# Requests for twelve weight loads moved to ScalarE's queue, and four splitting steps taken off VectorE

## The chip, the cores and the metric

The kernel runs on one core of a Trainium2 chip. The core has five engines that run side by side, each through its own list of instructions in order: TensorE (PE in the profile, its weight loads PEld), VectorE (DVE), ScalarE (ACT), GpSimd (POOL) and SyncE (SP), which here only requests transfers between the chip's memory and the on-chip memory. The metric is the device time of one execution in microseconds; lower is better.

## The reference

One layer of a bidirectional hybrid encoder over 512 tokens of width 1024. What matters here is the mixer: one combined input projection, whose columns feed a gated DeltaNet branch, an mLSTM branch and sigmoid gates.

```python
hn = rmsnorm(h_res, norm_mix_g) * (1.0 + sc1) + sh1        # 512 x 1024
proj = hn @ w_in                                           # 1024 x 6208 weights
a_qkv, a_z, a_gates, b_qk, b_v, b_o, b_gates, merge = split(proj)
...                                                        # DeltaNet: per chunk of 64 tokens, 8 heads
sol = triangular_solve(lower + eye, rhs, unit_diagonal=True)
...                                                        # o_a and h_b: the two branches
gate_a, gate_b = split(sigmoid(merge))                     # 2 x 1024 columns of proj
y = gate_a * (o_a @ w_branch_a) + gate_b * (h_b @ w_branch_b)
h_res = h_res + gt1 * (y @ w_out)
h_res = h_res + gt2 * hierarchical_moe(adaLN(h_res))       # 32 experts, 2 per token
```

All numbers are float32.

## The kernel before

The projection is worked in 48 tiles of 128 weight columns; a tile is named by its first column (w4416 is columns 4416 to 4543). For each tile `load_w` (L221 on) requests 512 KB of weights into a raw buffer (L224), splits them into a high part, rounded to TensorE's shorter float format (`move`, so L143 on ScalarE, L145 on VectorE or GpSimd), and a low part, raw minus high (`both`, L150). `proj_tile` (L340) then runs 24 matmuls of 512 columns: high weights by high inputs (L347), high by low (L348), low by high (L349). There are two raw, two high and two low buffers, so the request of a tile waits for the low part of the tile two before, and its high part waits for the matmuls of the tile two before.

A table of choices, `CHOICE`, says for each step which engine takes it: `hiw4672` is the high part of tile w4672, `low4672` its low part, "v" VectorE, "g" GpSimd, "a" ScalarE; a key that is missing takes the default, ScalarE for high parts and GpSimd for low parts. Every request for a load goes to SP's list.

A gate tile (`gate_tile`, L545) is a projection tile whose result goes through a tanh on ScalarE (L548, which frees one of the two PSUM accumulators) and is stored (L551) for later use. `GORDER` takes gate tiles 4 to 15 first: they are w4160, w4288, w4416, w4544, w4672, w4800, w4928, w5056, w5184, w5312, w5440 and w5568. In the program's text these twelve stand at the head of the part after the DeltaNet preparation, but a scheduler that works with estimated durations lists the instructions of each engine, and it mixes the twelve tiles with three other things:

- the end of the DeltaNet preparation: `vt` (L582), `gg` and `ib` (L671, L672), their stores `gd` and `iqd` (L673, L597), and the exchange, that is, transposes on TensorE (L608) whose results ScalarE and VectorE copy from PSUM into `kst` and `vp` (L143, L147);
- the triangular solve on VectorE: `gu` is loaded back from `gd` (L720), four steps make `nn` (L729, L731), then 31 pairs of a product into `gu` (L740) and an addition into `tt` (L742), and six transposes into `tw` (L752) end it;
- the modulation columns `mod_chunk`: weights `aw` (L781) by a per-partition scalar, added up in `ac` on VectorE (L788, L790), or, for one chunk here, on ScalarE (L786) and VectorE (L792 to L796); then a small matmul (L800) and a copy into `mcols` (L801).

After the solve come `bx` (L982, L983), the low part of w5696 on VectorE (L150), and with it TensorE's next projection tiles.

Of the kernel before, what the change touches and what calls it, by code (L numbers as in the profile page):

```python
# [110 lines left out]
def _body(tc, nc, ctx, ins, out, consts_in):  # L111
    V, A, G, PE, DMA = nc.vector, nc.scalar, nc.gpsimd, nc.tensor, nc.sync
    x, w_in, ada_w = ins["x"][0], ins["w_in"][0], ins["ada_w"][0]
# [13 lines left out]
    def ps(tag, shape=None):  # L127
        uid[0] += 1
        n, b = psum["tags"][tag]
        return psum["pool"].tile([128, n], F32, name=f"ps_{tag}{uid[0]}", tag=tag, bufs=b)  # L130
# [6 lines left out]
    def nb(key, default, *choices):  # L137
        return eng("#" + key, default, (default,) + choices)

    def move(key, dst, src, scale=None, default="a", choices="av"):  # L140
        e = eng(key, default, choices)
        if e == "a":
            A.activation(dst, src, AF.Copy, **({} if scale is None else {"scale": scale}))  # L143
        elif scale is None:
            ENGINE[e].tensor_copy(dst, src)  # L145
        else:
            ENGINE[e].tensor_scalar(dst, src, scale, None, op0=OP.mult)  # L147

    def both(key, dst, a, b, op, default="v", choices="vg"):
        ENGINE[eng(key, default, choices)].tensor_tensor(dst, a, b, op=op)  # L150
# [67 lines left out]

    RAWP = nb("wraw", 2, 3)

    def load_w(src, n, name, first=False):  # L221
        raw = ppr.tile([128, KD, 128], F32, name=name + "_raw", tag="wraw", bufs=RAWP)
        for (s, o, m) in src:
            DMA.dma_start(raw[:, :, o:o + m], s.rearrange("(k p) n -> p k n", p=128))  # L224
        if not first:
            hi = ppr.tile([128, KD, 128], F32R, name=name + "_hi", tag="whi", bufs=nb("whi", 2, 3))
            lo = ppr.tile([128, KD, 128], F32R, name=name + "_lo", tag="wlo", bufs=nb("wlo", 2, 3))
        else:
            hi, lo = (pf.tile([128, KD, 128], F32R, name=f"{name}_{i}") for i in range(2))
        move("hi" + name, hi[:, :, :n], raw[:, :, :n], choices="avg")  # L230
        both("lo" + name, lo[:, :, :n], raw[:, :, :n], hi[:, :, :n].bitcast(F32), OP.subtract, "g")
        return hi, lo
# [5 lines left out]
    def early_w(i):  # L238
        if i == 0:
            early[i] = load_w([(w_in[:, 2048:2080], 0, 32), (w_in[:, 4128:4160], 32, 32)], 64, "wg"), 64  # L240
        else:
            c0 = EARLY[i - 1]
            early[i] = load_w([(w_in[:, c0:c0 + 128], 0, 128)], 128, f"w{c0}", i > 1), 128
# [30 lines left out]
    for k in range(KD):  # L274
        p = ps("m")
# [48 lines left out]
    for nm, n in (("gdn_conv_w", 12), ("mlstm_conv_w", 8)):  # L324
        w = p0.tile([128, KD, 2, 256], F32, name="cwr" + nm, tag="adaw", bufs=3).rearrange("p k b n -> p (k b n)")
# [3 lines left out]
    p = ps("m")  # L329
# [7 lines left out]

    unprojected = [48]

    def proj_tile(c0):  # L340
        unprojected[0] -= 1
        if c0 in EARLY:
            return ep[1 + EARLY.index(c0)]
        hi, lo = load_w([(w_in[:, c0:c0 + 128], 0, 128)], 128, f"w{c0}")
        p = ps("acc")
        for k in range(KD):
            PE.matmul(p, hi[:, k], hn_hi[:, k], start=(k == 0), stop=False)  # L347
            PE.matmul(p, hi[:, k], hn_lo[:, k], start=False, stop=False)  # L348
            PE.matmul(p, lo[:, k], hn_hi[:, k], start=False, stop=(k == KD - 1))  # L349
        return p  # L350

    p = ep[0]
# [43 lines left out]
    p = ps("m")  # L396
# [13 lines left out]
    for c in range(2):  # L410
        p = ps("m")
# [17 lines left out]
    p = ps("m")  # L429
# [15 lines left out]
    for n in range(NCH):  # L445
        for d in range(2):
            i = n if d == 0 else NCH - 1 - n
# [95 lines left out]
    gts = dram("gts", [20, 128, S])  # L543

    def gate_tile(i):  # L545
        p = proj_tile(1536 + i * 128 if i < 4 else 4160 + (i - 4) * 128)
        th = cv.tile([128, S], F32, name=f"gt{i}", tag="ct", bufs=nb("ct", 2, 3))
        A.activation(th, p, AF.Tanh, scale=0.5)  # L548
        if i < 4:
            V.scalar_tensor_tensor(th, th, 1.0, p, op0=OP.add, op1=OP.mult)  # L550
        DMA.dma_start(gts[i], th)  # L551

    def gate_tiles():
        for i in GORDER:
            gate_tile(i)
            yield
# [66 lines left out]
    def gdn_pair(hp):  # L623
# [7 lines left out]
        for j, col0 in ((0, 512), (1, 0)):  # L631
            p = proj_tile(col0 + hp * 128)
            nm = f"{j}_{hp}"
            ac = conv_tile(p, (4 if j == 0 else 0) + hp, nm)
            silu2(kq[:, j], ac, nm)
            yield
# [44 lines left out]
    def gdn_value(hp):  # L681
        p = proj_tile(1024 + hp * 128)
        nm = f"v{hp}"
        ac = conv_tile(p, 8 + hp, nm)
        vt = pa.tile([128, S], F32, name=f"vt{hp}", tag="vt", bufs=nb("vt", 2, 3))
        silu2(vt, ac, nm)
        yield
        exchange(token_blocks(vt), put_scaled(vp[:, hp], 0.5, f"v{hp}"))
# [48 lines left out]
    for c in range(31):  # L737
        n, m = 31 - c, c + 1
        o = pd[:, :, :n * m].rearrange("p b (i j) -> p b i j", j=m)
# [9 lines left out]
    for i, (own, kind) in enumerate(((True, 0), (False, 1), (True, 1))):  # L749
        for d in range(2):  # L750
            m = tt[halves[d], d if own else 1 - d]
# [351 lines left out]
    p = ps("m")  # L1103
# [162 lines left out]
    def weight_tile(nm):  # L1266
        return pw.tile([128, 2048], F32, name="wr" + nm, tag="wraw", bufs=RAW)
# [84 lines left out]
    p = ps("m")  # L1352
# [8 lines left out]
    p = ps("m")  # L1361
# [163 lines left out]
    for i in range(2 * NT):  # L1525
        (c, t), (c1, t1) = divmod(i, NT), divmod(i - 1, NT)
        p = ps("acc")
# [146 lines left out]
    for i, (n, w) in enumerate(((64, 512), (64, 512), (32, 256), (32, 256), (32, 256), (32, 256))):  # L1674
        r, c, o = ((i, 0, i * 512) if i < 2 else (i - 2, 512, (i - 2) * 256))
# [79 lines left out]
    def t32(nm, n=32):  # L1755
        return px.tile([128, n], F32, name=nm)
# [4 lines left out]
    first = t32("first")  # L1761
# [185 lines left out]
    with tc.For_i(0, nblk, 1) as i:  # L1947
# [23 lines left out]
        c0 = t32("c0", NT)  # L1971
# [12 lines left out]
        raw = [weight_tile(f"v_{c}") for c in range(3)]  # L1984
# [14 lines left out]
        p = ps("m")  # L1999
# [4 lines left out]
        p = ps("d")  # L2004
# [88 lines left out]
```

## Time and profile before

| | us |
|---|---|
| median of 3 runs (lowest, highest) | 983.03 (981.76, 984.24) |
| the profiled execution, device time | 980.42 |
| its span in the profile | 978.6 |
| busy in the span: PE, DVE, ACT, POOL | 814.2, 660.8, 328.1, 316.6 |

The profile is of one execution and has the times of single instructions; the shares of busy time are averages over stages that differ much. The span is 1.8 us shorter than the device time of the same execution, and that execution was 2.6 us below the median of the three runs. Of the span, the part that the change touches lies between 140 and 290 us. Times in the views are microseconds from the start of the span.

### The profile page before, as it was taken

What the parts mean: (1) busy time and instruction counts of PE and PEld (TensorE: products, weight loads), DVE (VectorE), ACT (ScalarE), POOL (GpSimd) and SP (SyncE); (2) the same over time, 40 slices, a digit from 0 to 9 for tenths busy, and PEclk for the clock granted to TensorE, in tenths of its full rate; (3) what the DMA queues carried; (4) which work ended last, traced back from release to release, by engine and by line L of the source; (5) the groups of instructions that cost most, each with busy time, mean ns of one, the idle gap of its engine ahead of it and who ended that gap; (6) DMA issues with size and microseconds to landing.
All of it is one profiled execution on the core that took longest, in us unless ns stands there. A gap on an engine that the chain in (4) does not pass through costs nothing.

```text
span 978.6 us, 16538 instructions
## 1 busy us (share of the span) xinstructions
PE 814.2 (83%) x6204; PEld 595.0 (61%) x6204; DVE 660.8 (68%) x1246; ACT 328.1 (34%) x611; POOL 316.6 (32%) x236
## 2 busy tenths in 40 slices
PE   4799979979486999988797998987699999999840
PEld 3367656768375777866675776776456555555420
DVE  1459999799959999888888888459965322221215
ACT  5435475223101342321334231125522323333203
POOL 0321365214224442563236252323112212111125
PEclk9799999989786999998898999998899999999985
DMA  9932564975265365654474254946689999999965
GB/s 307 270 88 71 108 119 97 204 206 180 58 143 158 87 216 146 181 171 142 150 220 149 94 157 132 369 166 215 237 288 358 351 371 403 414 417 413 415 259 211
DMA packets 171709, 213.80 MB, mean 218 GB/s; under 512 B 47368, under 2 KB 129828, under 8 KB 171628
## 3 DMA queue, kind: packets, MB, share of 16 engines
q1 hardware_dynamic: 167340, 204.33, 64.6%
q0 software_dynamic: 4288, 8.41, 2.4%
q8 instruction: 49, 0.80, 0.3%
q14 instruction: 32, 0.26, 0.1%
HBM read 190.79 MB, written 25.54 MB: 221 GB/s over the span
## 4 chain that ended last, share of the span: by engine, by line
PE 41%; DVE 31%; DMA 16%; issue 5%; POOL 3%; ACT 2%; SPq 1%; POOLq 0%; DVEq 0%; ACTq 0%
DMA wr<-in_w_gate_dram 5%; PE ps_m L1705 5%; DMA wr<-in_w_up_dram 4%; PE ps_acc L348 3%; PE ps_acc L347 3%; PE ps_acc L349 3%; DMA wr<-in_w_down_dram 3%; DVE gu L740 2%; PE ps_m L1708 2%; PE ps_d L1736 2%; DVE ac L790 2%; DVE tt L742 2%; DVE ca L573 1%; PE ps_m L902 1%; DMA hb<-h1d 1%
## 5 line engine op out<-in xcount | busy, mean ns | idle before, releaser
L349 PE MATMUL ps_acc<-hn_hi,w_lo 128*128 128x512 f32 x352 | 142.6, 405 | 16.2 <-DVE w_lo L150 15.4
L347 PE MATMUL ps_acc<-hn_hi,w_hi 128*128 128x512 f32 x352 | 145.5, 413 | 1.8 <-DVE w_hi L145 1.3
L348 PE MATMUL ps_acc<-hn_lo,w_hi 128*128 128x512 f32 x352 | 145.0, 412 | 0.0
L1705 PE MATMUL ps_m<-wr,xin 128*64 128x256 f32 x1024 | 124.4, 390 | 6.1 <-ACT xin L1695 4.2
L150 POOL TENSOR_TENSOR w_lo<-w_raw,w_hi 128x1024 fp32r<-128x1024 f32 x34 | 88.1, 2590 | 103.2 <-ACT w_hi L143 80.9
L1714 DVE SCALAR_TENSOR_TENSOR act<-act,ps_m 64x256 f32<-64x256 f32 (+1 forms) x32 | 14.8, 463 | 133.0 <-ACT act L1713 133.0
L1705 PEld LDWEIGHTS ps_m<-wr,xin 128*64 128x64 f32 x1024 | 75.0, 139 | 43.3 <-issue 6.8
L349 PEld LDWEIGHTS ps_acc<-hn_hi,w_lo 128*128 128x128 f32 x352 | 68.7, 195 | 32.1 <-DVE w_lo L150 16.6
L347 PEld LDWEIGHTS ps_acc<-hn_hi,w_hi 128*128 128x128 f32 x352 | 68.8, 196 | 17.5 <-issue 3.2
L348 PEld LDWEIGHTS ps_acc<-hn_lo,w_hi 128*128 128x128 f32 x352 | 68.8, 195 | 15.6 <-issue 1.5
L1752 POOL DMA_INDIRECT ybuf<-y,idxp x28 | 27.3, 974 | 132.7 <-DVE y L1747 123.8
L1736 PE MATMUL ps_d<-wr,at 128*64 128x512 f32 x256 | 61.3, 598 | 5.2 <-DMA wr<-in_w_down_dram 4.0
L1695 ACT ACTIVATE xin<-xall (+1 forms) x128 | 54.2, 424 | 13.8 <-issue 9.5
L1713 ACT ACTIVATE act<-ps_m 64x256 f32<-64x256 f32 (+1 forms) x32 | 13.4, 418 | 134.7 <-PE ps_m L1705 71.1
L143 ACT ACTIVATE w_hi<-w_raw 128x1024 fp32r<-128x1024 f32 x30 | 31.7, 1058 | 57.3 <-PE ps_acc L348 43.5
L790 DVE SCALAR_TENSOR_TENSOR ac<-aw,cT,ac 128x256 f32<-128x256 f32 x77 | 44.0, 572 | 0.6
L1752 POOL DMA_INDIRECT ybuf<-y,idx x16 | 15.9, 992 | 74.6 <-DVE y L1747 61.1
L1747 DVE TENSOR_TENSOR y<-ps_d,gt 128x512 f32<-128x512 f32 (+1 forms) x32 | 25.3, 792 | 21.4 <-PE ps_d L1736 16.7
L1736 PEld LDWEIGHTS ps_d<-wr,at 128*64 128x64 f32 x256 | 17.4, 136 | 30.0 <-issue 20.1
L1725 PEld LDWEIGHTS ps_m<-ident,act 64*128 64x128 f32 x128 | 16.5, 186 | 22.4 <-DVE act L1715 12.6
L1497 PE MATMUL ps_acc<-woh,yT 128*128 128x512 f32 x64 | 27.5, 430 | 0.0
L740 DVE TENSOR_TENSOR gu<-nn,tt 128x62 f32<-128x62 f32 (+15 forms) x31 | 27.0, 870 | 0.7
(550 smaller groups left out, 1788.0 us busy)
## 6 DMA issues: line engine op xcount, KB each, us to landing
wr<-in_w_gate_dram SPq DMA_DIRECT2D x64, 512.0 KB
wr<-in_w_up_dram SPq DMA_DIRECT2D x64, 512.0 KB
wr<-in_w_down_dram SPq DMA_DIRECT2D x32, 1024.0 KB
w_raw<-in_w_in_dram SPq DMA_DIRECT2D x48, 512.0 KB
aw<-in_ada_w_dram SPq DMA_DIRECT2D x32, 512.0 KB
adaw<-in_ada_w_dram SPq DMA_DIRECT2D x8, 1024.0 KB
gts<-gt SPq DMA_DIRECT2D x20, 256.0 KB
gts<-gts SPq DMA_DIRECT2D x20, 256.0 KB
```

What stands on the lines that cost most here:

```text
L143: A.activation(dst, src, AF.Copy, **({} if scale is None else {"scale": scale}))
L150: ENGINE[eng(key, default, choices)].tensor_tensor(dst, a, b, op=op)
L347: PE.matmul(p, hi[:, k], hn_hi[:, k], start=(k == 0), stop=False)
L348: PE.matmul(p, hi[:, k], hn_lo[:, k], start=False, stop=False)
L349: PE.matmul(p, lo[:, k], hn_hi[:, k], start=False, stop=(k == KD - 1))
L740: V.tensor_tensor(o, nn_[:, :, m:, c].unsqueeze(3).to_broadcast([128, 2, n, m]), tt[:, :, c, 0:m].unsqueeze(2).to_broadcast([128, 2, n, m] ...
L790: V.scalar_tensor_tensor(acc, w[:, k], cT[:, kk:kk + 1], acc, op0=OP.mult, op1=OP.add)
L1497: PE.matmul(p, yT[0][:, k, ts], hi[:, k % 2], start=(k == 0), stop=False)
L1695: A.activation(xg[:, :, o], xall[:, :, bass.ds(vs[t], SEG)], AF.Copy)
L1705: PE.matmul(p[64 * b:64 * b + 64, 0:256], xg[:, kk, 0:64], r[:, b], **f)
L1736: PE.matmul(p[64 * c:64 * c + 64, 0:512], at[:, j, 0:64], w[:, j * D + c * 512:j * D + c * 512 + 512], start=(j == 0), stop=(j == 1))
L1752: return G.indirect_dma_start(out=ybuf.rearrange("r (a n) -> (r a) n", a=parts), out_offset=bass.IndirectOffsetOnAxis(ap=ix, axis=0), in_= ...
```

## The change

Twelve gate tiles, 4 to 15, hand `nc.scalar` down to `load_w`, so that their loads are requested from ScalarE's list in place of SP's. Four keys leave the table: `hiw4672` goes from VectorE to ScalarE, and `low4416`, `low4672` and `low4928` go from VectorE to GpSimd. One blank line is added in `gate_tile`, so lines from L546 on have a number higher by one in the changed kernel.

```diff
-    "hiw4544": "g", "hiw4672": "v", "hiw5824": "v", ...
+    "hiw4544": "g", "hiw5824": "v", ...
-    "low3744": "v", "low4416": "v", "low4672": "v", "low4928": "v", "low5696": "v", ...
+    "low3744": "v", "low5696": "v", ...
-    def load_w(src, n, name, first=False):
+    def load_w(src, n, name, first=False, queue=None):
...
-            DMA.dma_start(raw[:, :, o:o + m], s.rearrange("(k p) n -> p k n", p=128))
+            (queue or DMA).dma_start(raw[:, :, o:o + m], s.rearrange("(k p) n -> p k n", p=128))
...
-    def proj_tile(c0):
+    def proj_tile(c0, queue=None):
...
-        hi, lo = load_w([(w_in[:, c0:c0 + 128], 0, 128)], 128, f"w{c0}")
+        hi, lo = load_w([(w_in[:, c0:c0 + 128], 0, 128)], 128, f"w{c0}", queue=queue)
...
     def gate_tile(i):
-        p = proj_tile(1536 + i * 128 if i < 4 else 4160 + (i - 4) * 128)
+
+        p = proj_tile(1536 + i * 128 if i < 4 else 4160 + (i - 4) * 128, nc.scalar if 4 <= i < 16 else None)
```

The scheduler lists the instructions anew. ScalarE's list before, around the tanh of gate tiles 5 to 8 (gt5 to gt8; w4800_hi is a high part; kst an exchange copy):

```order
L548 ACTIVATE gt5_1693<-ps_acc78_1668 128x512
L548 ACTIVATE gt6_1727<-ps_acc79_1702 128x512
L548 ACTIVATE gt7_1761<-ps_acc80_1736 128x512
L143 ACTIVATE w4800_hi_1800<-w4800_raw_1798 128x1024
L143 ACTIVATE w4928_hi_1834<-w4928_raw_1832 128x1024
L548 ACTIVATE gt8_1795<-ps_acc81_1770 128x512
```

and the same place after:

```order
L549 ACTIVATE gt5_1693<-ps_acc78_1668 128x512
L224 DMA w4800_raw_1798<-in_w_in_dram 128x8x128
L143 ACTIVATE w4672_hi_1766<-w4672_raw_1764 128x1024
L224 DMA w4928_raw_1832<-in_w_in_dram 128x8x128
L143 ACTIVATE w4800_hi_1800<-w4800_raw_1798 128x1024
L224 DMA w5056_raw_1866<-in_w_in_dram 128x8x128
L549 ACTIVATE gt6_1727<-ps_acc79_1702 128x512
L549 ACTIVATE gt7_1761<-ps_acc80_1736 128x512
L143 ACTIVATE w4928_hi_1834<-w4928_raw_1832 128x1024
L549 ACTIVATE gt8_1795<-ps_acc81_1770 128x512
```

Three requests and the high parts of w4672 and w4800 now stand between the tanh of tile 5 and that of tile 6; each request waits for the low part of the tile two before it, and the two high parts wait for matmuls. VectorE's list before, in the first third of the solve (tt and gu are the solve's pairs, ac0 and ac1 the first two modulation sums, aw1_0 the weights of the second):

```order
L742 TENSOR_TENSOR tt_1516<-tt_1516,gu_1497 128x2x27x5
L801 COPY mcols_1592<-ps_m76_1624 128x2
L740 TENSOR_TENSOR gu_1497<-nn_1511,tt_1516 128x2x156
L145 CAST w4672_hi_1766<-w4672_raw_1764 128x1024
L742 TENSOR_TENSOR tt_1516<-tt_1516,gu_1497 128x2x26x6
L150 TENSOR_TENSOR w4672_lo_1767<-w4672_raw_1764,w4672_hi_1766 128x1024
L740 TENSOR_TENSOR gu_1497<-nn_1511,tt_1516 128x2x175
```

and after:

```order
L743 TENSOR_TENSOR tt_1516<-tt_1516,gu_1497 128x2x27x5
L802 COPY mcols_1592<-ps_m76_1624 128x2
L741 TENSOR_TENSOR gu_1497<-nn_1511,tt_1516 128x2x156
L789 TENSOR_SCALAR ac1_2415<-aw1_0_2416,cT_81 128x256
L743 TENSOR_TENSOR tt_1516<-tt_1516,gu_1497 128x2x26x6
L791 SCALAR_TENSOR_TENSOR ac1_2415<-aw1_0_2416,cT_81,ac1_2415 128x256
L741 TENSOR_TENSOR gu_1497<-nn_1511,tt_1516 128x2x175
L791 SCALAR_TENSOR_TENSOR ac1_2415<-aw1_0_2416,cT_81,ac1_2415 128x256
```

The two splitting steps of w4672 are gone from it, and the second modulation sum begins two and a half pairs of the solve sooner. GpSimd's list before, from the last product of the preparation (ib2) on:

```order
L150 TENSOR_TENSOR ib2_1386<-rb2_924,cst_72 128x512
L145 CAST w4544_hi_1732<-w4544_raw_1730 128x1024
L150 TENSOR_TENSOR w4544_lo_1733<-w4544_raw_1730,w4544_hi_1732 128x1024
L150 TENSOR_TENSOR w4800_lo_1801<-w4800_raw_1798,w4800_hi_1800 128x1024
L150 TENSOR_TENSOR w5056_lo_1869<-w5056_raw_1866,w5056_hi_1868 128x1024
```

and after:

```order
L150 TENSOR_TENSOR ib2_1386<-rb2_924,cst_72 128x512
L150 TENSOR_TENSOR w4416_lo_1699<-w4416_raw_1696,w4416_hi_1698 128x1024
L145 CAST w4544_hi_1732<-w4544_raw_1730 128x1024
L150 TENSOR_TENSOR w4544_lo_1733<-w4544_raw_1730,w4544_hi_1732 128x1024
L150 TENSOR_TENSOR w4672_lo_1767<-w4672_raw_1764,w4672_hi_1766 128x1024
L150 TENSOR_TENSOR w4800_lo_1801<-w4800_raw_1798,w4800_hi_1800 128x1024
L150 TENSOR_TENSOR w4928_lo_1835<-w4928_raw_1832,w4928_hi_1834 128x1024
L150 TENSOR_TENSOR w5056_lo_1869<-w5056_raw_1866,w5056_hi_1868 128x1024
```

The low parts of w4416, w4672 and w4928 are in it now, in the order of the tiles. From the solve's seventeenth pair on VectorE's list is as before, and in the program after the solve only one store stands one transfer sooner in SP's list.

## Rows read from the trace of the kernel before

**Rows 1.** Busy time of the engines in the stretch of the solve as a whole, and in stretches of 10 us at its end: stretch, its length, then PE, PEld, DVE, ACT and POOL busy with their numbers of instructions, the granted clock of TensorE as a share of full speed, the DMA engines' busy share, GB/s.
```profile
186.70:267.10 80.40, 63.48 (x270) 51.32 (x268) 78.10 (x97) 18.58 (x29) 24.46 (x10) 0.91 0.60 161
...
250.00:260.00 10.00, 5.67 (x26) 4.35 (x24) 9.50 (x16) 2.36 (x4) 0.00 (x0) 0.95 0.00 0
260.00:270.00 10.00, 0.00 (x0) 0.00 (x0) 9.87 (x7) 0.00 (x0) 2.75 (x6) 0.50 0.52 130
270.00:280.00 10.00, 9.14 (x29) 7.31 (x30) 7.70 (x8) 1.23 (x2) 3.48 (x2) 0.69 0.51 135
...
```

**Rows 2.** The chain of waits that ended last, in order of time, for 186 to 290 us: start, length of the piece, engine and line. The first three are the two splitting steps of w4672 and the low part of w4928; then the end of the solve and what follows it.
```profile
202.89 0.60 DVE w_hi L145
203.89 1.13 DVE w_lo L150
...
213.82 1.14 DVE w_lo L150
...
265.08 2.00 DVE tw L752
267.10 1.35 DVE bx L982
...
269.60 1.22 DVE w_lo L150
270.86 0.79 PE ps_acc L349
...
```

**Rows 3.** Timeline of TensorE around the end of the solve: start, duration, engine, line, operation, tiles, and in brackets the idle time ahead of it with what ended it.
```profile
255.28 0.39 PE L348 MATMUL ps_acc<-hn_lo,w_hi 128*128 128x512 f32 x1
270.86 0.79 PE L349 MATMUL ps_acc<-hn_hi,w_lo 128*128 128x512 f32 x1 [15.19 <-DVE w_lo L150]
```

**Rows 4.** Busy time by line on VectorE from 186.5 to 267.2 us, the stretch of the solve: line, operation, shapes, count, busy us, mean ns of one, idle us ahead with what ended it.
```profile
L740 DVE TENSOR_TENSOR gu<-nn,tt 128x62 f32<-128x62 f32 (+15 forms) x31 | 27.0, 870 | 0.7
L742 DVE TENSOR_TENSOR tt<-tt,gu 128x62 f32<-128x62 f32 (+15 forms) x31 | 21.3, 686 | 0.7
...
L801 DVE COPY mcols<-ps_m 128x2 f32<-128x2 f32 x1 | 0.2, 159 | 0.8 <-PE ps_m L800 0.8
```

**Rows 5.** Timeline of VectorE, columns as in Rows 3: a copy out of PSUM and a subtraction beside a low part on GpSimd; the preparation's last vt; the low part of w4416 and the last exchange copies; the first nn; and, inside the solve, steps beside GpSimd's low parts, with one of equal size that stands alone (222.43).
```profile
158.41 0.23 DVE L147 TENSOR_SCALAR vp<-ps_c 64x64 f32<-64x64 f32 x1
...
159.34 2.29 DVE L150 TENSOR_TENSOR rb<-rb,pk 128x1024 f32<-128x1024 f32 x1
...
172.12 1.55 DVE L582 SCALAR_TENSOR_TENSOR vt<-ctv,cav 128x512 f32<-128x512 f32 x1
...
177.57 1.21 DVE L150 TENSOR_TENSOR w_lo<-w_raw,w_hi 128x1024 fp32r<-128x1024 f32 x1
...
183.84 0.36 DVE L147 TENSOR_SCALAR kst<-ps_c 64x192 f32<-64x192 f32 x1 [0.81 <-PE ps_c L613]
186.73 6.62 DVE L729 SCALAR_TENSOR_TENSOR nn<-gu,bu 64x1024 f32<-64x1024 f32 x2 [2.53 <-DMA gu<-gd]
193.38 2.36 DVE L731 SCALAR_TENSOR_TENSOR nn<-gu,bu 64x1024 f32<-64x1024 f32 x2
...
219.63 2.76 DVE L740 TENSOR_TENSOR gu<-nn,tt 128x504 f32<-128x504 f32 x1
222.43 0.68 DVE L742 TENSOR_TENSOR tt<-tt,gu 128x504 f32<-128x504 f32 x1
...
229.21 2.88 DVE L740 TENSOR_TENSOR gu<-nn,tt 128x510 f32<-128x510 f32 x1
...
234.50 2.88 DVE L740 TENSOR_TENSOR gu<-nn,tt 128x494 f32<-128x494 f32 x1
```

**Rows 6.** Timeline of GpSimd, columns as in Rows 3: low parts of 128x1024.
```profile
158.16 2.38 POOL L150 TENSOR_TENSOR w_lo<-w_raw,w_hi 128x1024 fp32r<-128x1024 f32 x1 [1.11 <-ACT w_hi L143]
...
187.55 3.96 POOL L150 TENSOR_TENSOR w_lo<-w_raw,w_hi 128x1024 fp32r<-128x1024 f32 x1
...
219.22 2.63 POOL L150 TENSOR_TENSOR w_lo<-w_raw,w_hi 128x1024 fp32r<-128x1024 f32 x1 [11.97 <-ACT w_hi L143]
...
228.97 2.57 POOL L150 TENSOR_TENSOR w_lo<-w_raw,w_hi 128x1024 fp32r<-128x1024 f32 x1 [0.83 <-ACT w_hi L143]
234.47 2.39 POOL L150 TENSOR_TENSOR w_lo<-w_raw,w_hi 128x1024 fp32r<-128x1024 f32 x1 [2.92 <-ACT w_hi L143]
```

**Rows 7.** Timeline of SP's requests: start, time until the last of the group was requested, line, transfer, count. 174.30 and 181.32 are the stores of ib and the loads of gu; 190.28 and 198.53 the loads of w4672 and w4800; 199.01 the weights of the second modulation sum.
```profile
174.30 3.19 SPq L597 DMA_DIRECT2D iqd<-ib  x4
...
181.32 6.34 SPq L720 DMA_DIRECT2D gu<-gd  x8
...
190.28 0.90 SPq L224 DMA_DIRECT2D w_raw<-in_w_in_dram  x1
...
198.53 0.39 SPq L224 DMA_DIRECT2D w_raw<-in_w_in_dram  x1
199.01 2.60 SPq L781 DMA_DIRECT2D aw<-in_ada_w_dram  x2
```

**Rows 8.** Timeline of ScalarE, columns as in Rows 3: the tanh of gate tiles 4 and 6, and the high part of w4800.
```profile
176.79 0.58 ACT L548 ACTIVATE gt<-ps_acc 128x512 f32<-128x512 f32 x1
...
195.18 0.60 ACT L548 ACTIVATE gt<-ps_acc 128x512 f32<-128x512 f32 x1 [7.95 <-DMA gts<-gt]
...
203.24 1.06 ACT L143 ACTIVATE w_hi<-w_raw 128x1024 fp32r<-128x1024 f32 x1 [5.14 <-DMA w_raw<-in_w_in_dram]
```

4 rows, old and new, of the table CHOICE are left out of this document.

## The prediction, written before the changed kernel ran

> **What bounds the kernel now.** I read the busy time by stretch first, then the chain of waits, then the timelines of the engines that it names. Between 186.7 and 267.1 us VectorE is busy for 78.10 of 80.40 us; TensorE, which does the gate tiles there, is busy for 63.48, and has nothing at all from 260 to 270 us [rows 1]. The chain of waits for this stretch runs along VectorE's solve, through the transposes and `bx`, to one low part at 269.60 and only then back to TensorE at 270.86 [rows 2]. TensorE's own timeline says the same: it stood still for 15.19 us, and what ended that was the low part on VectorE [rows 3]. So in this stretch every microsecond that VectorE's list gets longer or shorter counts, and TensorE, the loads of gate weights and their queue have 15 us of room before they matter.
>
> The second thing to see is why VectorE's list is as long as it is. An addition of 128x504 alone takes 0.68 us (222.43). The product of the same size just ahead took 2.76 us, and two more of about that size 2.88 us each [rows 5]. Each of the three starts within half a microsecond of a low part on GpSimd (219.22, 228.97, 234.47) and ends shortly after it [rows 6]. So a low part on GpSimd holds up a VectorE instruction that reads two operands from on-chip memory by 2.76 - 0.68 = 2.08, 2.88 - 0.68 = 2.20 and again 2.20 us. It doesn't hold up all of them: beside the low part at 158.16 [rows 6] a copy out of PSUM took 0.23 us, while a subtraction with both operands in on-chip memory ended only with it, 2.29 us after its start [rows 5]. This is why the mean of the solve's products is 870 ns [rows 4].
>
> **The change, part by part.** I sum up how much later or sooner the solve ends, since what follows it hangs on it.
>
> *Taken off VectorE in the stretch.* On the chain the high part of w4672 has 0.60 us, its low part 1.13, and the low part of w4928 1.14 [rows 2]: 2.87 us less. The low part of w4416 (177.57, 1.21 us) is not in this sum: it lies ahead of the solve, where VectorE waits anyway, 2.53 us for `gu` alone at 186.73 [rows 5].
>
> *Put onto GpSimd in the stretch.* The low parts of w4672 and w4928 now meet the solve as the others do: VectorE's list there is nearly all products and sums from on-chip memory. Two times the mean of the three above, 2.16 us, makes 4.32 us more. From below the price is 0, if both fell beside copies out of PSUM as at 158.16. From above it is the dearest case in the trace: the two first `nn` took 6.62 us where the next two took 2.36 [rows 5], so 4.26 us went to a high part and a low part of GpSimd (187.55, 3.96 us, [rows 6]); if each new low part cost this, 8.5. I take 4.32, since the solve is the same kind of work as in the three rows. The low part of w4416 will run at about 177 to 180 us beside exchange copies out of PSUM: nothing, by the 0.23 us row.
>
> The Trainium skill, "SBUF — State Buffer", section "Who interferes with whom", says that a VectorE instruction with two inputs in SBUF and a GpSimd instruction that reads SBUF exclude each other for the length of a whole instruction, whichever starts first; by that the price of one would be GpSimd's whole 2.39 to 2.63 us [rows 6] and of both about 5.0. The rows have VectorE lose 2.1 to 2.2, as part of the low part overlaps the instruction already under way; the measured price stands, and this rule speaks against this part of the change either way.
>
> *High part on ScalarE.* One instruction of 1.06 us as at 203.24 [rows 8]. ScalarE is busy for 18.58 of the 80.40 us [rows 1], so its own time is hidden; if that cover were gone it would cost this 1.06.
>
> *Twelve requests on ScalarE.* The trace has no request on ScalarE. On SP one takes 0.39 us alone and up to 0.90 [rows 7], so 4.7 to 10.8 us of ScalarE's time for all twelve, spread over 110 us on an engine with three quarters of its time free: nothing by itself. What SP gains isn't on the chain: the loads are asked for sooner for some tiles (w4672 was requested at 190.28, behind the loads of `gu`, and can now go about 180) and TensorE may take its tiles a little sooner, inside its 15 us of room. What can cost is the wait: the request stands in ScalarE's list until the low part of two tiles before is done, and what is queued behind it waits too. Two places matter.
>
> First, before the solve. The request for w4672 follows the tanh of tile 4 (176.79 [rows 8]) and waits for the low part of w4416, which takes GpSimd about 2.4 us, as at 158.16 [rows 6]. The exchange copies stand behind it, and VectorE must do its own exchange copies (the last at 183.84) before the first `nn`. The 2.53 us wait for `gu` [rows 5] covers this. On the other side, the last product of `ib` comes ahead of the `vt` of 1.55 us [rows 5] instead of behind it, so SP can begin the chain of stores and loads, which ran nearly without a gap from 174.30 to the end of the `gu` loads at 187.66 [rows 7], up to 1.55 us sooner; but a product before it (`kq`) moves behind three others on VectorE, which hands back about 1.1. So the solve starts 0.4 us sooner; the ends are 1.55 sooner and 1.5 later (2.4 of wait and up to 1.6 of the others, less 2.5 of cover).
>
> Second, inside the solve. The tanh of tile 6 frees the accumulator that w4672 needs, and it now stands behind the requests for w4928 and w5056 and the high part of w4800. It ended at 195.8 before [rows 8]; I get about 202: matmuls of w4544 to 197, high part, low part of 2.6 us, request. The small matmul for `mcols` stands behind four matmuls of w4672, and VectorE waits for it; it waited 0.8 us before [rows 4]. With the new low part and that of w4800 ahead of it VectorE comes there some 4 us later, at about 205.5, so TensorE is ready just in time. The request for the second sum's weights waits on SP in the same knot and is needed 2.5 pairs sooner. I put 0.3 us for both waits, between 0 and 3.
>
> The sum: -2.87 + 4.32 - 0.4 + 0.3 = +1.35 us. After the solve the lists are the same, and TensorE, VectorE and the loads start from the solve's end, so I carry it to the end in full. Against the profiled execution that is 980.42 + 1.35 = 981.8 us; the median of the three runs is 2.6 above that execution, so 983.03 + 1.35 = 984.4 us.
>
> **The rivals.** Faster and slower mean beyond 0.3%, which is 2.95 us here and about what a measurement of this kernel can tell from no change.
>
> *The blocking isn't additive (faster).* If the two new low parts cost VectorE nothing, as beside the PSUM copies, the sum is -2.87 - 0.4 = -3.3, so 979.8 us. For it: 0.23 us at 158.41 [rows 5]. Against it: inside the solve there are no such copies but `mcols`, and each low part there shows as a step of 2.76 us or more.
>
> *ScalarE's waits come onto the chain (slower).* Place: the tanh of tile 6 behind the requests. Point: if it ends after about 203.4, TensorE's four matmuls and the `mcols` matmul end after VectorE gets there, and each further microsecond is one of the solve. Price: up to the 3 above in place of 0.3, and nothing in place of the -0.4 ahead of the solve: 1.45 + 3 = +4.45, so 987.5 us; with the exchange's 1.5 as well, 989.0. For it: the load of w4800 took 4.7 us from request to use before (198.53 [rows 7] to 203.24 [rows 8]), and the transfers there are dense. Against: it is requested 7 us sooner now.
>
> *The requests do nothing at all.* If they go out no sooner than from SP and wait where nothing hangs on it, only the four splitting steps are left: -2.87 + 4.32 = +1.45, so 984.5 us, the same to a measurement.
>
> **How the numbers follow.** The forecast has 0.66, the last rival 0.10, together 0.76 for the same; the faster rival 0.10; the slower 0.14. For the range I leave out most of the faster rival, since it lies at 979.8, and the far half of the slower: 980.5 to 987.2 us.
>
> **What would show it.** In the changed profile: VectorE between the first `nn` and the last transpose longer by 1 to 2 us, with two more products or additions of 2.7 us or more beside low parts; the first `nn` within a microsecond of 186.7; `mcols` with a wait below 1.5 us; the tanh of tile 6 near 202; TensorE still idle by 12 us or more before the low part of w5696. The prediction is wrong if steps beside the new low parts keep their 0.6 us, if VectorE waits more than 2 us for TensorE or for `aw` in the solve, or if the difference at the solve's end isn't the difference at the end of the span.

## The result, and the profile after

Over 20 runs each, the changed kernel has a median of 990.5 us and the kernel before 983.01, 7.5 us apart; the ratio is 1.0091, with a 95% interval of 1.0072 to 1.011. The ratio is of the fast runs alone (one run of the changed kernel, at 1177.63 us and a granted clock of 0.645, is not in it), so it is not the quotient of the two medians. So the change makes the kernel slower by about 0.9%, between 7 and 11 us, where I had forecast no change (984.4, at most 987.2). The profiled execution took 990.75 us; its span is 988.9, against 978.6 before.

The loss is made ahead of the solve. The first view is the timeline of VectorE in the changed kernel: start, duration, line, operation, tiles, and in brackets the idle time ahead with what ended it. (From line 546 on, lines are one higher than before.)

```profile
188.46 5.17 DVE L730 SCALAR_TENSOR_TENSOR nn<-gu,bu 64x1024 f32<-64x1024 f32 x2 [3.73 <-DMA gu<-gd]
201.77 2.36 DVE L732 SCALAR_TENSOR_TENSOR nn<-gu,bu 64x1024 f32<-64x1024 f32 x2 [8.14 <-DMA gu<-gd]
204.17 0.26 DVE L741 TENSOR_TENSOR gu<-nn,tt 128x62 f32<-128x62 f32 x1
...
206.13 0.35 DVE L789 TENSOR_SCALAR ac<-aw,cT 128x256 f32<-128x256 f32 x1 [1.40 <-DMA aw<-in_ada_w_dram]
...
212.22 0.16 DVE L802 COPY mcols<-ps_m 128x2 f32<-128x2 f32 x1 [0.77 <-PE ps_m L801]
...
262.64 11.73 DVE L753 STREAM_TRANSPOSE tw<-tt 64x1024 f32<-64x1024 f32 x6
274.40 1.34 DVE L983 TENSOR_SCALAR bx<-pk,cst 128x32 f32<-128x32 f32 x1
...
276.93 1.21 DVE L150 TENSOR_TENSOR w_lo<-w_raw,w_hi 128x1024 fp32r<-128x1024 f32 x1
```

The two first `nn` start at 188.46 instead of 186.73, 1.73 us late, and take 5.17 us instead of 6.62 [rows 5]. The other two, which followed without a gap before, now wait 8.14 us for `gu`. So the solve starts at 204.17 where 193.38 + 2.36 plus the step to the next instruction put it at about 195.8 before [rows 5]: 8.4 us late (1.73 - 1.45 + 8.14). Between there and `bx` the changed kernel wins 1.1 back: `bx` comes at 274.40 against 267.10 and the low part at 276.93 against 269.60, both 7.3 us late [rows 2].

What held `gu` is seen in SP's requests. In this timeline the second number is the time until the last request of the group was made.

```profile
183.06 2.47 SPq L721 DMA_DIRECT2D gu<-gd  x4
...
194.84 2.29 SPq L721 DMA_DIRECT2D gu<-gd  x4
201.60 0.95 SPq L782 DMA_DIRECT2D aw<-in_ada_w_dram  x2
204.69 0.34 SPq L552 DMA_DIRECT2D gts<-gt  x1
```

Before, the eight loads were requested in one row, from 181.32 to 187.66 [rows 7]. Now four go out, SP stands still for 9.3 us, and four more follow. The list of what SP waited for from 170 to 215 us (line that waited, what ended it, us in total, times, longest) names the cause; before, no row of this list had a load of weights in it:

```profile
SPq L721 <- DMA w_raw<-in_w_in_dram: 9.3, 1, 9.3
SPq L782 <- DMA w_raw<-in_w_in_dram: 4.4, 1, 4.4
...
SPq L598 <- DMA w_raw<-in_w_in_dram: 2.1, 1, 2.1
SPq L552 <- DMA w_raw<-in_w_in_dram: 2.1, 1, 2.1
SPq L674 <- DMA w_raw<-in_w_in_dram: 1.8, 1, 1.8
```

A load of `gu` waits for a load of gate weights, with which it shares no data. The listing of the changed kernel tells why. It gives the transfers of SP and ScalarE eight completion semaphores in turn, in the order of one common list, and a request that gets a used semaphore first waits until the transfer that had it before has landed. These are rows of SP with the semaphores that each waits for, and two of ScalarE:

```
(SP)      96 L721 DMA gu_1497<-gd_648 32x32x32 [waits DMAHW2_49,DMAHW0_49]
(SP)      97 L721 DMA gu_1497<-gd_648 32x32x32 [waits DMAHW1_49]
(SP)      98 L721 DMA gu_1497<-gd_648 32x32x32 [waits DMAHW3_49]
(SP)      99 L721 DMA gu_1497<-gd_648 32x32x32 [waits DMAHW5_49]
(SP)     100 L721 DMA gu_1497<-gd_648 32x32x32 [waits DMAHW6_49]
(ScalarE) 144 L224 DMA w4800_raw_1798<-in_w_in_dram 128x8x128 [waits DMAHW6_49,DMAHW2_49,Pool_49]
(ScalarE) 147 L143 ACTIVATE w4800_hi_1800<-w4800_raw_1798 128x1024 [waits DMAHW6_49,PE_49]
```

Semaphore 6 belongs to the load of w4800, and eight transfers later in the list to the fifth load of `gu`. Now the timeline of ScalarE (ACTq marks a request), and the low part on GpSimd that frees the buffer:

```profile
177.83 0.37 ACTq L224 DMA_DIRECT2D w_raw<-in_w_in_dram  x1
...
189.82 0.37 ACTq L224 DMA_DIRECT2D w_raw<-in_w_in_dram  x1
191.63 1.06 ACT L143 ACTIVATE w_hi<-w_raw 128x1024 fp32r<-128x1024 f32 x1 [4.62 <-PE ps_acc L348]
195.87 0.39 ACTq L224 DMA_DIRECT2D w_raw<-in_w_in_dram  x1
...
200.63 0.38 ACTq L224 DMA_DIRECT2D w_raw<-in_w_in_dram  x1
```

```profile
187.40 2.39 POOL L150 TENSOR_TENSOR w_lo<-w_raw,w_hi 128x1024 fp32r<-128x1024 f32 x1
```

The request for w4800 needs the buffer that this low part (w4544) reads to 189.79. It goes out at 189.82, and at 194.84, 5.0 us later, SP goes on with the fifth load of `gu`. The first load of `aw` (201.60) and the first store of `gts` (204.69) stand in the same way behind the loads of w4928 (195.87) and w5056 (200.63), and follow those requests by 5.7 and 4.1 us. While all these requests stood on SP, the transfer eight places back had always been requested; on two queues it may be one that the other engine can't make yet. The stores ahead of `gu` (lines 598 and 674 in the list of waits) lost 2.1 and 1.8 us in the same way, and the first `nn` came 1.73 late.

### The profile page after: what moved, and what is told of

It is laid out like the page before. It is cut to its first block, busy times and chain, and to the rows that moved or that the text cites. A ratio compares the mean times of both kernels' runs of the same rounds, so it can differ in the third digit from the quotient of the medians.

```text
span 988.9 us, 16544 instructions
## 1 busy us (share of the span) xinstructions
PE 818.0 (83%) x6204; PEld 597.8 (60%) x6204; DVE 656.4 (66%) x1242; ACT 328.6 (33%) x612; POOL 323.8 (33%) x239
## 5 line engine op out<-in xcount | busy, mean ns | idle before, releaser
L150 POOL TENSOR_TENSOR w_lo<-w_raw,w_hi 128x1024 fp32r<-128x1024 f32 x37 | 93.4, 2525 | 106.8 <-ACT w_hi L143 81.9
L791 DVE SCALAR_TENSOR_TENSOR ac<-aw,cT,ac 128x256 f32<-128x256 f32 x77 | 48.3, 628 | 0.6
L1726 PEld LDWEIGHTS ps_m<-ident,act 64*128 64x128 f32 x128 | 16.5, 186 | 23.4 <-DVE act L1716 12.6
L1499 PE MATMUL ps_acc<-wol,yT 128*128 128x512 f32 x64 | 26.5, 414 | 0.1
```

The lines of the kernel that those rows point to most:

```text
L791: V.scalar_tensor_tensor(acc, w[:, k], cT[:, kk:kk + 1], acc, op0=OP.mult, op1=OP.add)
L1499: PE.matmul(p, yT[0][:, k, ts], lo[:, k % 2], start=False, stop=False)
```

## The experiments

All expectations below stood before the runs. Times are compared with runs of the kernel before on the same chip, 981.75 us in the first group of four kernels and 980.14 in the second. I took theory A (the shared completion semaphore) against two others: B, the low parts moved to GpSimd block VectorE; C, the loads of `gu` are slow because 512 KB loads are in flight beside them.

**The requests alone.** The four entries of the table are put back, so VectorE does its splitting steps as before; the requests stay on ScalarE.

```
+    ... "hiw4672": "v", ... "low4416": "v", "low4672": "v", "low4928": "v", ...
```

> The twelve loads are requested from ScalarE as in the changed kernel, and the four splitting steps stand where they stood before. Theory A (shared completion semaphore): the requests of SP and ScalarE take eight completion semaphores in turn, in the order of the list, and a request waits until the transfer that had its semaphore before it has landed; so the fifth load of gu waits for the load of w4800, which ScalarE can request only when GpSimd has freed a buffer, near 190 us. Then the eight loads of gu again take 12 to 15 us from the first request to the last, VectorE waits 7 to 9 us for gu, and the solve starts near 204 us; the time is 988 to 991. Theory B (the splitting steps moved to GpSimd block VectorE): nothing of them is moved here, so the time is that of before, 982 to 984, and the solve starts near 196 us.

Measured: 993.16 us, ratio 1.0104 (1.0055 to 1.0154). SP's requests and VectorE:

```profile
184.92 14.63 SPq L721 DMA_DIRECT2D gu<-gd  x8
```

```profile
194.78 4.00 DVE L730 SCALAR_TENSOR_TENSOR nn<-gu,bu 64x1024 f32<-64x1024 f32 x2
202.60 2.36 DVE L732 SCALAR_TENSOR_TENSOR nn<-gu,bu 64x1024 f32<-64x1024 f32 x2 [3.82 <-DMA gu<-gd]
204.99 0.26 DVE L741 TENSOR_TENSOR gu<-nn,tt 128x62 f32<-128x62 f32 x1
```

The eight loads take 14.63 us and the solve starts at 204.99, as A has it, with no low part moved to GpSimd. So B can't be the cause of the late start. In this kernel SP waits three times for a load of weights ahead of a load of `gu`, 12.0 us in all: the fifth load of `gu` (195.51) follows the request for w4800 (191.03) by 4.5 us, and the eighth, at 199.25, stands eight places behind w4928. The wait that VectorE shows for `gu` is 3.82 us and not 7 to 9, because its own splitting steps of w4672 stand ahead of the first `nn` here, and VectorE had waited 6.90 us for TensorE to free a buffer for them (until 192.84). The median is above the 988 to 991 that I gave A. The profiled execution took 996.6 us: it lost 4.7 us more near 510 us, in a stretch in which TensorE's granted clock was 0.57 (508 to 518 us), that is mostly the lower level of 1.2 GHz, where the same work had 1.00, 2.4 GHz, before (500 to 510). In the 10 us ahead TensorE was busy for 8.76 at 0.75 here and for 8.77 at 0.83 before, so what made the clock fall is not seen in these rows.

**The splitting steps alone**, and once more in more rounds. The kernel before, without the four entries; all loads requested from SP.

```
-    ... "hiw4672": "v", ... "low4416": "v", "low4672": "v", "low4928": "v", ...
```

> All loads are requested from SP as before; only the three low parts and one high part are off VectorE. Theory A: no request of SP shares a semaphore with a load that ScalarE has yet to request, the eight loads of gu take 6 to 7 us, the solve starts near 196 us, and what is left is the trade in the solve, 2.87 us of steps removed against at most 4.3 us of blocking: 981 to 985. Theory B: the whole loss is here, 988 to 991, with the solve starting near 196 us and more steps of 2.7 us in it.

> The kernel with the splitting steps alone once more, in more rounds, because its first profile and its first times point to different places. Reading of its first profile: the solve starts and ends some 1.7 us earlier than before, and then 5.3 us are lost because the low part of w2080 stands behind cb on GpSimd; so the first mb is 3 to 4 us later than before and the time is 985 to 989. If the first times were chance, it is 981 to 984.

Measured: 988.97 us, ratio 1.01 (1.0037 to 1.0163), and the second time 988.76, ratio 1.0086 (1.0052 to 1.0119). Theory A's figure of 981 to 985 was a miss, and the time is inside B's range; but the profiles show no loss in B's place. Both profiles have the loads of `gu` in 6.3 and 6.6 us, and from the first product of the solve to its first transpose it is 59.3 us in both, 0.2 less than before. What these profiles do lose lies behind it, on GpSimd (second profile):

```profile
267.93 1.26 POOL L150 TENSOR_TENSOR cb<-gg,cst 128x512 f32<-128x512 f32 x1 [16.98 <-DVE tw L752]
269.14 2.34 POOL L150 TENSOR_TENSOR w_lo<-w_raw,w_hi 128x1024 fp32r<-128x1024 f32 x1
271.44 1.30 POOL L150 TENSOR_TENSOR cb<-gg,cst 128x512 f32<-128x512 f32 x1
```

In this kernel's list the masking step `cb` stands ahead of the low part of w2080, not behind it. GpSimd waits 16.98 us ahead of `cb`, until the solve's transposes (`tw`) end, with that low part behind; what `cb` needs of them is not shown. TensorE then does w2080 after the solve and not in its idle time, and the first `mb` comes 28.0 us after `bx` where it came 23.8 after it before (267.10 to 290.85). But that does not account for the 0.9%. The first `mb` is 3.5 and 5.0 us late in the two profiles (294.38 and 295.86), and most of this is made up again between 440 and 466 us: the step `cs` (L860), at 486.64 before, comes at 488.46 and 488.56. The first profiled execution took 983.82 us, the fastest of four, and the second 979.83, the fastest of eight and faster than that of before. So the splitting steps by themselves also lose by the medians, and a swap in GpSimd's list delays what follows the solve; that the one makes the other is not shown.

**One store more.** The changed kernel with one of the stores between w4800's place in the list and the loads of `gu` cut in two; no byte is added.

```
-            DMA.dma_start(iqd[:, d, hh, r0:r0 + 64, hp]..., src[halves[hh]])
+            dst_ = iqd[:, d, hh, r0:r0 + 64, hp]...
+            for a, b in ((0, 4), (4, 8)) if hp == 2 and d == 1 and hh == 1 and not swap else ((0, 8),):
+                DMA.dma_start(dst_[:, a:b], src[halves[hh], a:b])
```

> The changed kernel, with one of the stores that stand in SP's list between the load of w4800 and the first load of gu cut in two halves; no byte more is moved. Theory A: the eighth transfer after the load of w4800 is now the fourth load of gu and not the fifth, so SP requests three loads, then waits until about 194.8 us; the first of the four steps that make nn needs the first four loads and starts at 197 to 200 us instead of 188.5, and the solve starts 1 to 4 us later than in the changed kernel: 990 to 994. Theory C (the loads of gu are slow because the 512 KB loads are in flight beside them): one cut store changes nothing, five or four loads are requested at the same times as before, the first step of nn starts near 188.5 us, and the time is that of the changed kernel, 990.5 within 1.

Measured: 990.71 us, ratio 1.009 (1.0051 to 1.0129). SP's requests and VectorE (lines are 2 higher):

```profile
185.23 1.81 SPq L723 DMA_DIRECT2D gu<-gd  x3
...
196.25 5.10 SPq L723 DMA_DIRECT2D gu<-gd  x5
```

```profile
190.07 2.96 DVE L732 SCALAR_TENSOR_TENSOR nn<-gu,bu 64x1024 f32<-64x1024 f32 x1 [3.94 <-DMA gu<-gd]
199.03 1.88 DVE L732 SCALAR_TENSOR_TENSOR nn<-gu,bu 64x1024 f32<-64x1024 f32 x1 [6.00 <-DMA gu<-gd]
204.22 2.36 DVE L734 SCALAR_TENSOR_TENSOR nn<-gu,bu 64x1024 f32<-64x1024 f32 x2 [3.32 <-DMA gu<-gd]
```

Three loads go out, then SP waits, and the fourth follows 5.0 us after ScalarE's request at 191.22. The gap has moved by exactly one load, as A says and C can't. I had one thing wrong: the first `nn` needs only the first and third load and starts at 190.07; the second `nn` is the one that waits. The solve starts at 206.61, 2.4 us later than in the changed kernel, inside A's 1 to 4. The total doesn't tell A from C, but the place of the gap does.

**The same loads from GpSimd.** In the listing, transfers requested there have semaphores of their own.

```
-        p = proj_tile(..., nc.scalar if 4 <= i < 16 else None)
+        p = proj_tile(..., nc.gpsimd if 4 <= i < 16 else None)
```

> The changed kernel with the twelve loads requested from GpSimd in place of ScalarE; GpSimd's transfers have completion semaphores of their own. Theory A: the 512 KB loads are in flight at about the same times, but no load of gu waits for one: the eight requests follow each other within 6 to 9 us, VectorE waits less than 4 us for gu in all, and the solve starts by 198 us. GpSimd now also issues twelve loads (estimate 1 us each, from 0.99 us for one of its indirect transfers in the profile), which can delay its low parts: 982 to 988. Theory C: bytes in flight are what slows the loads of gu, so VectorE waits 7 us or more for gu as in the changed kernel, and the time is 989 to 993.

Measured: 984.12 us, ratio 1.0027 (0.9997 to 1.0058). VectorE:

```profile
189.46 4.68 DVE L730 SCALAR_TENSOR_TENSOR nn<-gu,bu 64x1024 f32<-64x1024 f32 x2 [5.51 <-DMA gu<-gd]
194.17 4.39 DVE L732 SCALAR_TENSOR_TENSOR nn<-gu,bu 64x1024 f32<-64x1024 f32 x2
198.60 0.26 DVE L741 TENSOR_TENSOR gu<-nn,tt 128x62 f32<-128x62 f32 x1
```

The eight requests take 8.86 us and the second pair of `nn` doesn't wait. The wait ahead of the first is 5.51 us, above the 4 that I gave A, and the solve starts at 198.60 instead of by 198; 2.8 us late instead of 8.4. No row of SP's waits names a load of weights here. The solve itself is slower in this profile, 61.4 us from its first product to its first transpose (260.01) where it was 59.55, so `bx` is 4.7 us late (271.76); the median doesn't show it.

**Part of the loads on ScalarE.** Three kernels that differ from the changed one only in which tiles ask on ScalarE. First all but w4800, w4928 and w5056:

```
-        p = proj_tile(..., nc.scalar if 4 <= i < 16 else None)
+        p = proj_tile(..., nc.scalar if 4 <= i < 9 or 12 <= i < 16 else None)
```

> The changed kernel, with the loads of w4800, w4928 and w5056 requested from SP again (the other nine from ScalarE; the splitting steps as in the changed kernel). Theory A (shared completion semaphore): no load of gu and no load of aw comes eight transfers behind a load that ScalarE has yet to request, so the eight loads of gu are requested within 6 to 9 us, VectorE waits less than 4 us for gu, the solve starts at 195 to 198 us, and the low part of w2080 stands ahead of the masking step cb on GpSimd, so that nothing is lost behind the solve either: 981 to 985. Theory B (low parts on GpSimd block VectorE): the solve starts in time but takes 3 to 5 us longer, 987 to 990.

Measured: 982.13 us, ratio 1.0023 (0.9994 to 1.0053); no difference from before that can be told, and by the two ratios 0.7% less than the changed kernel.

```profile
183.52 6.14 SPq L721 DMA_DIRECT2D gu<-gd  x8
```

```profile
188.50 6.13 DVE L730 SCALAR_TENSOR_TENSOR nn<-gu,bu 64x1024 f32<-64x1024 f32 x2 [2.77 <-DMA gu<-gd]
194.66 4.40 DVE L732 SCALAR_TENSOR_TENSOR nn<-gu,bu 64x1024 f32<-64x1024 f32 x2
199.09 0.26 DVE L741 TENSOR_TENSOR gu<-nn,tt 128x62 f32<-128x62 f32 x1
```

The eight loads go out in one row again, though nine of the twelve weight loads and all four splitting steps are as in the changed kernel. The solve starts at 199.09, a microsecond behind what I expected of A: the first `nn` is 1.77 us late (0.85 us of it is there at 122 us, ahead of any moved request, and the first load of `gu` still waits 1.8 us for that of w4672, eight places ahead), and the second pair now meets a low part and takes 4.40 us. From there to the first transpose (257.95) it is 58.9 us, less than the 59.55 before, so B's 3 to 5 us are not there.

Then only the last six tiles, and only the first six:

```
+        ... nc.scalar if 10 <= i < 16 else None)
+        ... nc.scalar if 4 <= i < 10 else None)
```

> The changed kernel with only the last six of the twelve loads (w4928 to w5568) requested from ScalarE. Theory A: the loads of gu are free of waits and the solve starts near 196 us; but the list puts the low part of w2080 behind the masking step cb on GpSimd, as in the kernel with the splitting steps alone, and cb waits for the last transposes of the solve; so that low part starts after 264 us, TensorE does one more tile behind the solve, and the first mb comes 28 to 30 us after bx instead of 23.8: 985 to 990. If the place in GpSimd's list did not matter, the time would be 982 to 985.

> The changed kernel with only the first six of the twelve loads (w4160 to w4800) requested from ScalarE. Theory A: the eighth transfer behind the load of w4800 is now the seventh load of gu, so six loads of gu are requested in a row and the last two near 195 us; no load from ScalarE is in flight beside these two, the second pair of nn starts at 197.5 to 199.5 us and the solve at 200 to 202, and the low part of w2080 stands ahead of cb: 985.5 to 989. Theory C (bytes in flight): w4672 and w4800 are in flight beside gu as in the changed kernel, so the second pair of nn starts near 201.8 and the time is 989 to 991.

Last six: 994.11 us, ratio 1.0116 (1.0065 to 1.0166), above the expected 985 to 990. The loads of `gu` and GpSimd's list are as expected: solve from 195.9 us, then on GpSimd

```profile
268.49 1.29 POOL L150 TENSOR_TENSOR cb<-gg,cst 128x512 f32<-128x512 f32 x1 [16.45 <-DVE tw L753]
269.71 2.37 POOL L150 TENSOR_TENSOR w_lo<-w_raw,w_hi 128x1024 fp32r<-128x1024 f32 x1
```

and the first `mb` 28.5 us after `bx`, 6.0 us late in all. The profile ends 12.6 us behind that of before. Of the rest, 4.7 us are lost at the place where the kernel with the requests alone lost them: the first `cs` (L861) is 6.6 us late at 493.24 and an addition into `tot` 11.3 late at 518.23, with a granted clock of 0.50 from 505 to 515 us. What made the clock fall, and what makes the last 2 us, I did not find. First six: 986.27 us, ratio 1.0054 (1.0021 to 1.0086), inside A's range. SP requests six loads in a row, and two after the gap:

```profile
187.08 4.42 SPq L721 DMA_DIRECT2D gu<-gd  x6
...
199.37 0.91 SPq L721 DMA_DIRECT2D gu<-gd  x2
```

The count is A's: the seventh load is the eighth transfer behind w4800, and follows ScalarE's request (193.84) by 5.5 us. The start times were a miss: all of it lies about 4 us later than in the changed kernel, and the solve starts at 206.9 instead of 200 to 202. Most of this is not of the change: the copy `mc` (L509) comes at 125.75 instead of 121.91 already, and the first moved request goes out at 153.10. So by the profiles the places of the gap hold in four kernels (fourth load with one store more, fifth in the changed one and with the requests alone, seventh here), and the gap is gone wherever no load of `gu` but the first has such a partner.

## Why the prediction was wrong

**What failed** is the third term, "So the solve starts 0.4 us sooner", with its ends of 1.55 sooner and 1.5 later. The first `nn` came 1.73 later, just past that end, and the first product 8.4 later: for a wait of VectorE between the two pairs of `nn`, 8.14 us, the sum had no term, though it was to give the end of the solve. The term priced what ScalarE's wait does to ScalarE's own list and the cover that the wait for `gu` gives, and took the loads of `gu` themselves to be as before, or a little sooner, because SP had less in its list. It did not ask what SP's requests wait for. The rows that carry a request's waits were to be had from the listing without any run, and a request of the other queue stands in them.

**What held, and what did not.** The splitting steps are gone from the solve, and TensorE was idle 16.03 us until the low part of w5696, where I asked for 12 or more:

```profile
278.20 0.79 PE L349 MATMUL ps_acc<-hn_hi,w_lo 128*128 128x512 f32 x1 [16.03 <-DVE w_lo L150]
```

`mcols` waited 0.77 us, below the 1.5 that I set, and `aw` cost 1.40, below 2. Two signs were missed: the first `nn` was to come within a microsecond of 186.7, and the stretch from it to the last transpose was to be 1 to 2 us longer, where it is 5.6. One sign of being wrong came true in the profiles: the difference at the solve's end is 7.3 us, 5.8 near 560 us and 10.3 at the end. Why it comes and goes by some 3 us stays open. Single executions differ by as much: the profile of the kernel with three tiles on SP ends 6.2 us behind that of before, while its median doesn't differ, and 4.7 of these arise between 487 and 513 us, at a granted clock of 0.53 from 500 to 510.

**What was mis-sized.** First and second term together were +1.45 us for the trade in the solve. In the changed kernel the low parts of w4672 and w4800 (192.77 and 198.26) fell into the wait for `gu` and cost next to nothing, and only that of w4928 (219.21) met an addition, of 2.70 us, so it doesn't test the sum. The two runs with the steps alone give -0.2, but there the low part of w2080 had left the solve. The kernel with three tiles on SP has all of it: from first `nn` to first transpose 69.45 us (188.50 to 257.95) against 68.60 before (186.73 to 255.33), so +0.85, where first, second and fourth term together had +1.75. In these single profiles the sign was right and the size off by 0.9. One reading was a little high: steps beside low parts in the trace before took 2.64 (246.21) to 2.88 us, not 2.76 or more.

**The rivals.** The slower one, "ScalarE's waits come onto the chain", had the right source but the wrong place, and with 989.0 the nearest time by luck: the tanh of tile 6 did come late (208.32 instead of about 202), and nobody on VectorE waited for it, since VectorE was later still. Nor was it the list that ended this tanh's wait:

```profile
208.32 1.28 ACT L549 ACTIVATE gt<-ps_acc 128x512 f32<-128x512 f32 x2 [10.20 <-DMA gts<-gt]
```

It waited for the store of an earlier tanh, which SP could request only at 204.69, behind the load of w5056. The way from ScalarE's wait to VectorE runs over SP.

Of the 8.14 us, the held request is the larger part. The loads in flight add some: from the last request of `gu` to the second pair of `nn` it is 2.35 us with only the first six tiles on ScalarE (200.28 to 202.63), where w4928 isn't in flight, and 4.64 in the changed kernel (197.13 to 201.77), where it was requested at 195.87. That this 2.3 is due to the load is argued from these two rows, not shown by itself.

## What to carry to other kernels

Before transfers are moved to a second queue, look in the listing at what the requests behind them wait for: with a few completion semaphores dealt out in turn, a load that its new engine can only request late holds up whichever transfer comes a full turn behind it, however unrelated. Move only loads whose request can go out at once, or leave room for the turn; here three tiles put back on SP took the loss away as far as the runs can tell (1.0023, 0.9994 to 1.0053). And a change that shortens one engine's list can swap two steps of another's, so compare every engine's list around the places where it waits.

## What the runs showed that I had not expected

A 512 KB load took 5.0 us from ScalarE's request to the release of SP at the changed kernel's 189.82, 5.0 at 191.22 with one store more, 5.5 at 193.84 with the first six tiles, and 4.5 at 191.03 with the requests alone; this is the length by which a held request is late, on top of the wait for the buffer. The same twelve loads requested from GpSimd cost the kernel nothing that these runs can tell (1.0027, 0.9997 to 1.0058). And the splitting steps alone, a change of four table entries, lose about 0.9% by the medians, as much as the whole change; their profiles show one swap in GpSimd's list, with which the first `mb` comes 4.2 to 5.3 us further behind `bx`, and leave the rest open.
